# Modulation vectors of a two-layer hybrid block: row products on TensorE replaced by elementwise sums on VectorE and GpSimd and one-column products

## The chip, the cores and the metric

The kernel runs on one core of one Trainium2 chip. The metric is the device time of one execution in microseconds. A core has these engines: TensorE (PE, with its weight loads shown apart as PEld), VectorE (DVE), ScalarE (ACT), GpSimd (POOL) and SyncE (SP, which here issues DMAs). Each works through its own list of instructions in order and waits on semaphores of the others.

## What is computed

Two layers of a hybrid backbone over 1024 latent tokens and 256 context tokens, model width 1024. Each layer has modulation vectors, an input projection, four token mixers, a gated merge of their outputs, an output projection and a layer norm. The parts that matter here are the modulation and the merge:

```python
def modulation(cond, w_mod, b_mod):
    mod = jax.nn.silu(cond) @ w_mod + b_mod
    return jnp.split(mod, 3, axis=-1)

def merge_branches(ys, z, m, w_branch, w_out):
    ...
    acc = sum(jax.nn.sigmoid(ms[i]) * ((ys[i] * jax.nn.silu(zs[i])) @ w_branch[i]) for i in range(N_BRANCH))
    return acc @ w_out

    shift, scale, gate = modulation(c[:, None, :], w_mod, b_mod)
    shift_c, scale_c, gate_c = modulation(c_ctx, w_mod, b_mod)
    p_lat = (layer_norm(x) * (1.0 + scale) + shift) @ w_in
    ...
    x_new = layer_norm(DEEPNORM_ALPHA * x + gate * out) * ln_g + ln_b
```

`w_mod` is 1024 x 3072 per layer, in float32, and there are two condition rows: `c` for the latent tokens and `c_ctx` for the context. The product is thus of two rows by a matrix of 12 MB per layer.

## The kernel before

Shift and scale of layer 0 are needed at the very start and are computed there. The rest is done later, by a generator `later_mods` (L1161): the gate of layer 0 (1024 columns), shift and scale of layer 1 (2048 columns) and the gate of layer 1 (1024 columns). `later_mods` is woven by `weave` (L83, called at L1008) into the merge of layer 0, the stage whose tiles have the prefix `merge`: `weave` takes the next step of the stream that is least far along by its count of steps, 96 for the merge and 68 for the modulations. The merge of layer 1 has no such stream beside it.

**The old modulation** (`modulation`, L173). Each step loads a block of `w_mod`, 128 rows by 512 columns, 256 KB, into a tile with the tag `q` (three buffers). TensorE multiplies it by the two columns of `sc` for these rows (the SiLU of the conditions, 128 rows by 2), with `sc` as weights, in four column groups (L188). The eight row blocks accumulate in PSUM, in the tile `mod__pm`. There the result lies as two rows by many columns. So at the end ScalarE copies each piece to SBUF (L194), TensorE transposes it by 128 columns (L197), and VectorE adds the bias (L199). The tile `modc` then has one column per 128 channels for each condition.

**The merge** (`merge`, L979). The four branches come in the order 2, 3, 1, 0. For each there are eight column blocks c of 128 channels, and for each of those three token groups of 256, 512 and 512. A step multiplies the branch's input u by a 256-row piece of `w_branch` into one third of the PSUM tile `wide`. Where c is even, the gate's logits are computed by TensorE as well (`mm_b`, L307 to L309, three fp32r products for one f32 product: high by high, high by low, low by high). Where c is odd, they were computed earlier and are loaded (L992, `merge__tmp<-start__gates`). ScalarE takes the sigmoid (L996), VectorE multiplies (L1002), and the product is added into the accumulator `acc` (L1003), by GpSimd where c is odd and by VectorE where it is even.

The input u of a branch is loaded in six pieces (`load_u`, L963, with the DMA at L973): two column blocks by three token groups. The pieces land in tiles of the pool `tmp`, which the merge's gates and products use too, so a load waits until such a tile is released; ScalarE and VectorE split each piece into a high and a low part (`hi_lo`, L312 and L313: `merge__uh`, `merge__ul`).

**What sets the order.** Within an engine the program's order is decided when the kernel is built, by a scheduler that places the instructions of the woven streams by when it expects their inputs and their tiles to be free. Nearly all loads here are issued by SyncE, in one queue in program order: a load that waits for its tile holds up those behind it. After the merge, the gate of layer 0 is written to DRAM by two scatter DMAs (L1014, `last__gate<-mod__modc`), and these too are placed among the merge's loads, as soon as the gate is there.

## Time and profile before

| | us |
|---|---|
| median of three runs | 2957.4 (2956.92 to 2962.73) |
| profiled execution | 2960.92 |
| its span | 2959.1 |
| TensorE busy in the span | 2790.4 (94%) |
| VectorE, ScalarE | 1508.0 (51%), 1219.0 (41%) |
| GpSimd | 418.8 (14%) |
| mean granted clock of TensorE | 0.977 |

TensorE is the engine that is busy nearly all the time. A busy engine's own list decides the time only where it doesn't stop, so the stretch of the merge of layer 0 (from about 1090 to 1504 us) is read by itself. In the group rows the last part of a line is the time that the engine stood idle just before these instructions, with what ended it. In the timeline that is the bracket. In the windows a granted clock of 1.00 is TensorE's full speed.

### The profile page before, as it was taken

The page shows a single profiled execution, that of the slowest core. Times are in us where ns is not written, and L with a number is a line of the kernel's source. Part 1 is how long each engine was busy: PE and PEld are TensorE (multiplying, and loading weights), DVE is VectorE, ACT ScalarE, POOL GpSimd, SP SyncE. Part 2 cuts the span into 40 slices and gives each one's busy share as a digit, 9 for nine tenths or more (in the row PEclk, how much of TensorE's full clock was granted, in tenths as well). Part 3 has the DMA queues.
Part 4 walks back from the last instruction along what each step waited for, and adds up shares of the span by engine and source line. Part 5 has one row for each costly group of instructions (what it writes and reads, how often), then busy time and mean ns, then how long its engine had stood idle before and what let it go on. Part 6 is the DMA issues. An engine that isn't in the chain of part 4 may idle for free.

```text
span 2959.1 us, 40218 instructions
## 1 busy us (share of the span) xinstructions
PE 2790.4 (94%) x14458; PEld 2253.0 (76%) x14458; DVE 1508.0 (51%) x3069; ACT 1219.0 (41%) x2631; POOL 418.8 (14%) x507
## 2 busy tenths in 40 slices
PE   7997979999999999899999798999999999999998
PEld 3785858888888887677767576778888888777776
DVE  5644266555555552232458554356555556533456
ACT  4344256445455542222234434346545455522230
POOL 1210020110111100111222120012111111001131
PEclk9998989999999999999999898999999999999999
DMA  6333322222223333333332333423222323222232
GB/s 248 115 107 102 107 72 84 84 84 87 88 88 123 103 98 111 104 120 104 124 98 90 91 103 111 117 74 102 80 93 78 106 103 126 87 94 87 86 109 91
DMA packets 240424, 301.83 MB, mean 102 GB/s; under 512 B 27488, under 2 KB 160096, under 8 KB 240224
## 3 DMA queue, kind: packets, MB, share of 16 engines
q1 hardware_dynamic: 134368, 225.58, 24.2%
q10 hardware_dynamic: 105856, 73.68, 8.0%
q8 instruction: 114, 1.87, 0.3%
q14 instruction: 86, 0.70, 0.1%
HBM read 217.11 MB, written 82.07 MB: 101 GB/s over the span
## 4 chain that ended last, share of the span: by engine, by line
PE 75%; DVE 7%; DMA 4%; ACT 4%; issue 2%; POOL 2%; ACTq 1%; SPq 0%; DVEq 0%; POOLq 0%
PE wide L639 6%; PE merge__mm L307 4%; PE merge__mm L308 4%; PE merge__mm L309 4%; PE wide L307 3%; PE wide L308 3%; PE wide L309 3%; PE m_att__t L584 3%; PE g_att__t L584 2%; PE a_att__mm L307 2%; PE a_att__mm L308 2%; PE a_att__mm L309 2%; PE m_att__mm L309 2%; PE m_att__mm L308 2%; PE m_att__mm L307 2%
## 5 line engine op out<-in xcount | busy, mean ns | idle before, releaser
L307 PE MATMUL merge__mm<-xh,merge__whi 128*128 128x512 f32 (+1 forms) x640 | 243.0, 380 | 0.9 <-ACT a_att__tmp L934 0.9
L308 PE MATMUL merge__mm<-xl,merge__whi 128*128 128x512 f32 (+1 forms) x640 | 239.6, 374 | 0.0
L309 PE MATMUL merge__mm<-xh,merge__wlo 128*128 128x512 f32 (+1 forms) x640 | 239.4, 374 | 0.0
L313 DVE TENSOR_TENSOR m_att__pl<-m_att__t,m_att__ph 128x384 fp32r<-128x384 f32 (+1 forms) x248 | 122.1, 508 | 117.2 <-ACT m_att__ph L312 78.8
L263 ACT CAST merge__whi<-merge__wraw 128x256 fp32r<-128x256 f32 (+1 forms) x128 | 65.6, 513 | 255.6 <-PE merge__mm L308 176.7
L1002 DVE TENSOR_TENSOR merge__tmp<-wide,merge__tmp 128x512 f32<-128x512 f32 (+1 forms) x120 | 76.5, 637 | 184.8 <-PE wide L309 161.2
L1003 POOL TENSOR_TENSOR merge__acc<-merge__acc,merge__tmp 128x512 f32<-128x512 f32 (+1 forms) x60 | 79.2, 1320 | 585.9 <-DVE merge__tmp L1002 585.8
L307 PEld LDWEIGHTS merge__mm<-xh,merge__whi 128*128 128x128 f32 x640 | 120.6, 188 | 44.5 <-issue 19.9
L312 ACT CAST m_att__ph<-m_att__t 128x384 fp32r<-128x384 f32 (+1 forms) x248 | 105.0, 439 | 115.3 <-PE m_att__t L584 103.5
L313 DVE TENSOR_TENSOR g_att__pl<-g_att__t,g_att__ph 128x384 fp32r<-128x384 f32 (+1 forms) x228 | 111.3, 514 | 79.6 <-ACT g_att__ph L312 58.4
L307 PE MATMUL wide<-merge__uh,merge__whi 128*128 128x256 f32 (+1 forms) x320 | 127.4, 398 | 20.4 <-ACT merge__uh L312 11.5
L264 DVE TENSOR_TENSOR merge__wlo<-merge__wraw,merge__whi 128x256 fp32r<-128x256 f32 (+1 forms) x128 | 71.0, 555 | 141.2 <-ACT merge__whi L263 134.3
L309 PEld LDWEIGHTS merge__mm<-xh,merge__wlo 128*128 128x128 f32 x640 | 120.8, 189 | 23.9 <-issue 0.4
L308 PEld LDWEIGHTS merge__mm<-xl,merge__whi 128*128 128x128 f32 x640 | 120.8, 189 | 22.3
L312 ACT CAST g_att__ph<-g_att__t 128x384 fp32r<-128x384 f32 (+1 forms) x228 | 97.7, 446 | 69.3 <-PE g_att__t L584 65.3
L307 PE MATMUL a_att__mm<-xh,a_att__whi 128*128 128x512 f32 (+1 forms) x320 | 123.8, 387 | 0.0
L641 DVE TENSOR_SCALAR_CACHE_REDUCE m_att__p<-wide 128x1280 f32<-128x1280 f32 (+1 forms) x72 | 98.7, 1371 | 42.1 <-PE wide L639 41.8
L309 PE MATMUL a_att__mm<-xh,a_att__wlo 128*128 128x512 f32 (+1 forms) x320 | 120.1, 377 | 0.0
L639 PE MATMUL wide<-g_att__ks,g_att__q 128*128 128x512 f32 (+1 forms) x400 | 103.5, 365 | 17.5 <-DVE g_att__p L641 16.3
L308 PE MATMUL a_att__mm<-xl,a_att__whi 128*128 128x512 f32 (+1 forms) x320 | 120.0, 375 | 0.0
L299 PE MATMUL a_proj__mm<-a_proj__whi,xh 128*128 128x256 f32 (+1 forms) x320 | 112.0, 351 | 8.1 <-ACT a_proj__tmp L809 4.5
L308 PE MATMUL wide<-merge__ul,merge__whi 128*128 128x256 f32 (+1 forms) x320 | 119.6, 374 | 0.0
(418 smaller groups left out, 7919.4 us busy)
## 6 DMA issues: line engine op xcount, KB each, us to landing
merge__wraw<-in_w_chunks_dram SPq DMA_DIRECT2D x64, 256.0 KB, 2.9
mod__wm<-in_w_mod_dram SPq DMA_DIRECT2D x64, 256.0 KB, 3.0
g_proj__wm<-in_w_mod_dram SPq DMA_DIRECT2D x16, 512.0 KB, 9.8
a_att__wraw<-in_w_chunks_dram SPq DMA_DIRECT2D x32, 256.0 KB, 2.7
merge__wraw<-in_w_branch_dram SPq DMA_DIRECT2D x64, 128.0 KB, 2.1
merge__tmp<-start__gates SPq DMA_DIRECT2D x32, 256.0 KB, 3.2
merge__tmp<-outp__gates SPq DMA_DIRECT2D x32, 256.0 KB, 3.4
g_att__wraw<-in_w_chunks_dram SPq DMA_DIRECT2D x28, 256.0 KB, 2.7
```

The source lines that it names most:

```text
L264: (pool if by_pool else dve).tensor_sub(lo[:, :n], raw[:, :n], hi[:, :n])
L299: pe.matmul(ps, xh, wh[:, n0:n1], start=first and k == 0, stop=False)
L307: pe.matmul(ps, wh, xh, start=first and k == 0, stop=False)
L308: pe.matmul(ps, wh, xl, start=False, stop=False)
L309: pe.matmul(ps, wl, xh, start=False, stop=last and k == nk - 1)
L312: act.copy(hi, src)
L313: dve.tensor_sub(lo, src, hi)
L584: pe.transpose(tb[:, i * 128:(i + 1) * 128], pts[q0 + i][:, col:col + 128], ident)
L639: pe.matmul(wide[:, c0:c0 + w], qs[:, j, qi * 128:(qi + 1) * 128], k[:, c0:c0 + w], start=j == 0, stop=j == len(ks) - 1)
L641: dve.tensor_scalar(pt[:, :nk], wide[:, :nk], -scale, None, ALU.mult, ALU.min, accum_out=nb)
L1002: dve.tensor_mul(sgm[:, :g[1]], pb[:, :g[1]], sgm[:, :g[1]])
L1003: (pool if w is None else dve).tensor_add(acc[c][:, gs], acc[c][:, gs], sgm[:, :g[1]])
```

## The change

`later_mods` calls a new function, `modulation_apart`, for all three. The same blocks of `w_mod` are loaded, in another order: now all eight row blocks of 512 columns, then the next 512 columns. Each is multiplied by one number per row (the SiLU of the condition for that row) and the eight products are summed element by element. VectorE does that for the first condition in one instruction per block (L225), GpSimd for the second in two, a scaling into the tile `rb` and an add (L227, L228). The sum over the 128 rows is then left to TensorE: each 128 columns of the sum are the weights of one product with a single column of constants −0.5 (L233), whose result is one column in PSUM, already as `modc` wants it. VectorE multiplies by −2 and adds the bias (L236). The two sums use tiles that other stages own, `ph` with three buffers and `pl` with two. The stream now has 75 steps in place of 67, and its count in `weave` is 76 in place of 68. Lines behind the new function are 36 higher in the new kernel: L973 is L1009, L992 is L1028, L1003 is L1039 and L1014 is L1050.

```diff
@@ -199,6 +199,42 @@
         dve.tensor_tensor(mc[:, :, :n].rearrange("p s n -> p n s"),
                           tps[:, :2 * n].rearrange("p (n s) -> p n s", s=2),
                           bm[:, :n, None].to_broadcast([128, n, 2]), ALU.add)
+        if n == 16:
+            dve.tensor_scalar(mc[:, :, 8:16], mc[:, :, 8:16], 1.0, None, ALU.add)
+        out["m"] = mc
+        yield
+
+    def raw_w():
+        return tp.tile([128, 512], F32, tag="q", name=nm("wm"), bufs=3)
+
+    def modulation_apart(l, base, ncols, out):
+
+        acc = ps_v.tile([128, 512], F32, tag="pv", name=nm("pm"))
+        n = ncols // 128
+        bm = lc.tile([128, 16], F32, tag="bm", name=nm("bm"))
+        sp.dma_start(bm[:, :n], a["b_mod"][l, :, base // 128:base // 128 + n])
+        for h in range(ncols // 512):
+            sums = [tp.tile([128, 512], F32, tag=tag, name=nm("ms"), bufs=b) for tag, b in (("ph", 3), ("pl", 2))]
+            for k in range(KC):
+                w = raw_w()
+                sp.dma_start(w, a["w_mod"][l, k * 128:(k + 1) * 128, base + h * 512:base + (h + 1) * 512])
+                if k == 0:
+                    dve.tensor_scalar(sums[0], w, sc[:, k, 0:1], None, ALU.mult)
+                    pool.tensor_scalar(sums[1], w, sc[:, k, 1:2], None, ALU.mult)
+                else:
+                    dve.scalar_tensor_tensor(sums[0], w, sc[:, k, 0:1], sums[0], ALU.mult, ALU.add)
+                    p = tp.tile([128, 512], F32, tag="rb", name=nm("mp"), bufs=1)
+                    pool.tensor_scalar(p, w, sc[:, k, 1:2], None, ALU.mult)
+                    pool.tensor_tensor(sums[1], sums[1], p, ALU.add)
+                yield
+            for s in range(2):
+                for c in range(4):
+                    o = s * n + 4 * h + c
+                    pe.matmul(acc[:, o:o + 1], sums[s][:, c * 128:(c + 1) * 128], mhalf[:, 0:1], start=True, stop=True)
+            yield
+        mc = lc.tile([128, 2, 16], F32, tag="modc", name=nm("modc"), bufs=4)
+        dve.scalar_tensor_tensor(mc[:, :, :n], acc[:, :2 * n].rearrange("p (s n) -> p s n", s=2), -2.0,
+                                 bm[:, None, :n].to_broadcast([128, 2, n]), ALU.mult, ALU.add)
         if n == 16:
             dve.tensor_scalar(mc[:, :, 8:16], mc[:, :, 8:16], 1.0, None, ALU.add)
         out["m"] = mc
@@ -1005,7 +1041,7 @@
 
         for _ in fill["gen"]:
             pass
-        weave((f"merge{l}", merge(), 4 * KC * len(qgroups)), (f"mod{l}", side, 68))
+        weave((f"merge{l}", merge(), 4 * KC * len(qgroups)), (f"mod{l}", side, 76))
 
 
         phase[0] = f"last{l}"
@@ -1155,13 +1191,10 @@
     ctx.push(pools)
     x1 = dr.tile([SEQ, D], F32, name="x1", bufs=1)
 
-    def raw_w():
-        return tp.tile([128, 512], F32, tag="q", name=nm("wm"), bufs=3)
-
     def later_mods():
-        yield from modulation(0, 2048, 1024, gate0, raw_w, 512)
-        yield from modulation(1, 0, 2048, mc1, raw_w, 512)
-        yield from modulation(1, 2048, 1024, gate1, raw_w, 512)
+        yield from modulation_apart(0, 2048, 1024, gate0)
+        yield from modulation_apart(1, 0, 2048, mc1)
+        yield from modulation_apart(1, 2048, 1024, gate1)
 
     def fin0(t, Y, later):
         if t >= CT:
```

Three places show how the order moves. The first is GpSimd at the last boundary between two branches of the merge: before, its list there holds the accumulator adds of column blocks 5 and 7 of the third branch and nothing else.

```order
L1003 TENSOR_TENSOR merge__acc_11450<-merge__acc_11450,merge__tmp_12922 128x256
L1003 TENSOR_TENSOR merge__acc_11450<-merge__acc_11450,merge__tmp_12936 128x512
L1003 TENSOR_TENSOR merge__acc_11450<-merge__acc_11450,merge__tmp_12947 128x512
L1003 TENSOR_TENSOR merge__acc_11624<-merge__acc_11624,merge__tmp_13096 128x256
L1003 TENSOR_TENSOR merge__acc_11624<-merge__acc_11624,merge__tmp_13135 128x512
L1003 TENSOR_TENSOR merge__acc_11624<-merge__acc_11624,merge__tmp_13153 128x512
```

Now the scalings (L227) and adds (L228) of the last sum, `ms_13692`, stand between the adds into the accumulator of column block 7 (`acc_11668`). The sum's first scaling (L223) and one add are ahead of the excerpt. L223 waits until TensorE has read the sum two before it, whose buffer this sum takes.

```order
L228 TENSOR_TENSOR mod__ms_13692<-mod__ms_13692,mod__mp_13770 128x512
L227 TENSOR_SCALAR mod__mp_13846<-mod__wm_13843,sc 128x512
L1039 TENSOR_TENSOR merge__acc_11668<-merge__acc_11668,merge__tmp_13255 128x256
L228 TENSOR_TENSOR mod__ms_13692<-mod__ms_13692,mod__mp_13846 128x512
L227 TENSOR_SCALAR mod__mp_13869<-mod__wm_13866,sc 128x512
L228 TENSOR_TENSOR mod__ms_13692<-mod__ms_13692,mod__mp_13869 128x512
L1039 TENSOR_TENSOR merge__acc_11668<-merge__acc_11668,merge__tmp_13269 128x512
L227 TENSOR_SCALAR mod__mp_13886<-mod__wm_13883,sc 128x512
L228 TENSOR_TENSOR mod__ms_13692<-mod__ms_13692,mod__mp_13886 128x512
L227 TENSOR_SCALAR mod__mp_13903<-mod__wm_13900,sc 128x512
L228 TENSOR_TENSOR mod__ms_13692<-mod__ms_13692,mod__mp_13903 128x512
L1039 TENSOR_TENSOR merge__acc_11668<-merge__acc_11668,merge__tmp_13289 128x512
```

The three adds into `acc_11668` followed each other directly; now more than two steps of the modulation stand ahead of the first of them, and one and a half to two between each and the next.

The second is SyncE's queue at the same boundary, with the loads of u for the last branch (`start__u_23`). Before, two modulation loads stand between the first and the second piece, and the rest of u follows together.

```order
L992 DMA merge__tmp_13135<-start__gates_18_120 128x512
L992 DMA merge__tmp_13153<-start__gates_18_120 128x512
L973 DMA merge__tmp_13166<-start__u_23_125 128x256
L185 DMA mod__wm_13340<-in_w_mod_dram 128x512
L185 DMA mod__wm_13355<-in_w_mod_dram 128x512
L973 DMA merge__tmp_13170<-start__u_23_125 128x512
L973 DMA merge__tmp_13174<-start__u_23_125 128x512
L973 DMA merge__tmp_13180<-start__u_23_125 128x256
L278 DMA merge__wraw_13505<-in_w_branch_dram 128x256
L973 DMA merge__tmp_13184<-start__u_23_125 128x512
L973 DMA merge__tmp_13188<-start__u_23_125 128x512
```

Now modulation loads stand ahead of the first and behind it, and other loads lie between the pieces; each modulation load waits for the scaling by GpSimd of the block three before it.

```order
L220 DMA mod__wm_13866<-in_w_mod_dram 128x512
L1028 DMA merge__tmp_13289<-start__gates_18_120 128x512
L314 DMA merge__wraw_13532<-in_w_branch_dram 128x256
L220 DMA mod__wm_13883<-in_w_mod_dram 128x512
L1009 DMA merge__tmp_13302<-start__u_23_125 128x256
L220 DMA mod__wm_13900<-in_w_mod_dram 128x512
L220 DMA mod__wm_13994<-in_w_mod_dram 128x512
L1009 DMA merge__tmp_13306<-start__u_23_125 128x512
L171 DMA outp__gt_14159<-last__gate_14084 128x1024
L1009 DMA merge__tmp_13310<-start__u_23_125 128x512
L1009 DMA merge__tmp_13316<-start__u_23_125 128x256
```

The third is SyncE's queue at the first boundary, where the branch after it gets its u (`start__u_26`). Before, the gate's scatter stands between the second and the third piece.

```order
L973 DMA merge__tmp_11680<-start__u_26_128 128x256
L973 DMA merge__tmp_11684<-start__u_26_128 128x512
L180 DMA mod__bm_13147<-in_b_mod_dram 128x8
L1014 DMA last__gate_13919<-mod__modc_11666 128x8x1 x2
L278 DMA merge__wraw_12015<-in_w_branch_dram 128x256
L973 DMA merge__tmp_11688<-start__u_26_128 128x512
L973 DMA merge__tmp_11694<-start__u_26_128 128x256
L973 DMA merge__tmp_11698<-start__u_26_128 128x512
L185 DMA mod__wm_11869<-in_w_mod_dram 128x512
L973 DMA merge__tmp_11702<-start__u_26_128 128x512
```

Now the scatter has moved behind all six, and ahead of the weights and gate logits of the following column block.

```order
L1009 DMA merge__tmp_11725<-start__u_26_128 128x256
L220 DMA mod__wm_12491<-in_w_mod_dram 128x512
L314 DMA merge__wraw_12073<-in_w_branch_dram 128x256
L220 DMA mod__wm_12587<-in_w_mod_dram 128x512
L1009 DMA merge__tmp_11729<-start__u_26_128 128x512
L1009 DMA merge__tmp_11733<-start__u_26_128 128x512
L220 DMA mod__wm_12628<-in_w_mod_dram 128x512
L215 DMA mod__bm_13281<-in_b_mod_dram 128x8
L220 DMA mod__wm_12669<-in_w_mod_dram 128x512
L1050 DMA last__gate_14084<-mod__modc_11697 128x8x1 x2
L314 DMA merge__wraw_12126<-in_w_chunks_dram 128x512
L1028 DMA merge__tmp_11887<-start__gates_11_113 128x256
```

The scatter went from the middle of the u loads to the head of the loads behind them.

## Rows read from the trace of the kernel before

**Rows 1.** Stretches: length, busy PE, PEld, DVE, ACT, POOL (instructions), clock, DMA share, GB/s
```profile
1092.00:1504.00 412.00, 396.97 (x1950) 295.20 (x1950) 143.68 (x246) 111.01 (x236) 57.03 (x52) 0.99 0.38 116
1203.00:1210.00 7.00, 6.50 (x19) 4.48 (x19) 3.43 (x7) 2.51 (x6) 0.00 (x0) 0.66 0.18 54
```

**Rows 2.** Groups by line and shape, TensorE, 1030 to 1510 us; last a weight load
```profile
L188 PE MATMUL mod__pm<-mod__wm,sc 128*2 128x512 f32 x64 | 22.5, 592 | 0.0
L307 PE MATMUL wide<-merge__uh,merge__whi 128*128 128x256 f32 x64 | 20.7, 324 | 13.9 <-ACT merge__uh L312 8.8 <-DVE merge__tmp L1002 5.1
L188 PE MATMUL mod__pm<-mod__wm,sc 128*2 128x256 f32 x128 | 18.7, 378 | 0.0
...
L584 PE MATMUL a_att__t<-ident,a_att__pa 128*128 128x128 f32 x64 | 11.8, 278 | 0.0
...
L197 PE MATMUL mod__t<-ident,mod__tmp 2*128 2x2 f32 x32 | 3.7, 204 | 1.1 <-ACT mod__tmp L194 1.1
...
L309 PEld LDWEIGHTS merge__mm<-xh,merge__wlo 128*128 128x128 f32 x378 | 71.5, 189 | 12.4 <-issue 0.4
```

**Rows 3.** TensorE's timeline around one group of old products: start, duration, [idle before]
```profile
1181.63 0.39 PE L308 MATMUL wide<-merge__ul,merge__whi 128*128 128x512 f32 x1
1181.86 0.39 PE L309 MATMUL wide<-merge__uh,merge__wlo 128*128 128x512 f32 x1
1182.17 0.60 PE L188 MATMUL mod__pm<-mod__wm,sc 128*2 128x256 f32 x4
1182.70 0.39 PE L307 MATMUL merge__mm<-xh,merge__whi 128*128 128x256 f32 x1
```

**Rows 4.** DMA issues, 1186 to 1210 us: count, KB each, us to landing
```profile
last__gate<-mod__modc SPq DMA_DIRECT2D x2, 4.0 KB, 11.1
```

**Rows 5.** Timeline around the long stop: SyncE's queue, then TensorE
```profile
1189.37 1.16 SPq L1014 DMA_DIRECT2D last__gate<-mod__modc  x2
...
1191.89 1.69 SPq L973 DMA_DIRECT2D merge__tmp<-start__u  x3
...
1203.49 0.58 PE L307 MATMUL wide<-merge__uh,merge__whi 128*128 128x256 f32 x1 [7.65 <-ACT merge__uh L312]
```

**Rows 6.** DMA issues, 1280 to 1310 us (the next branch)
```profile
merge__tmp<-start__u SPq DMA_DIRECT2D x4, 256.0 KB, 3.1
```

**Rows 7.** TensorE's timeline: f32 transposes of 128x128, then of two rows
```profile
802.88 0.49 PE L584 MATMUL m_att__t<-ident,m_att__p 128*128 128x128 f32 x3
...
1396.47 0.40 PE L197 MATMUL mod__t<-ident,mod__tmp 2*128 2x2 f32 x4
```

**Rows 8.** Groups by line and shape, GpSimd, whole span
```profile
L1003 POOL TENSOR_TENSOR merge__acc<-merge__acc,merge__tmp 128x512 f32<-128x512 f32 x48 | 70.3, 1465 | 275.4 <-DVE merge__tmp L1002 275.3
...
L264 POOL TENSOR_TENSOR a_att__wlo<-a_att__wraw,a_att__whi 128x512 fp32r<-128x512 f32 x32 | 41.3, 1291 | 2.8 <-PE m_att__mm L309 0.3
...
L261 POOL CAST m_att__whi<-m_att__wraw 128x512 fp32r<-128x512 f32 x28 | 17.1, 611 | 295.6 <-PE m_att__mm L308 176.6 <-PE g_att__mm L308 119.0
```

**Rows 9.** Groups by line and shape, VectorE, 1030 to 1510 us
```profile
L466 DVE SCALAR_TENSOR_TENSOR a_att__y<-a_att__y,a_att__tmp 128x512 f32<-128x512 f32 x2 | 1.4, 692 | 0.1
```

**Rows 10.** Timeline: GpSimd and VectorE at the same time
```profile
1487.98 2.03 POOL L1032 TENSOR_TENSOR xl<-merge__acc,xh 128x256 fp32r<-128x256 f32 x2 [1.20 <-ACT xh L1031]
...
1488.19 1.22 DVE L1003 TENSOR_TENSOR merge__acc<-merge__acc,merge__tmp 128x512 f32<-128x512 f32 x1
```

**Rows 11.** Timeline of the last branch boundary: TensorE, GpSimd, TensorE
```profile
1395.67 0.28 PE L307 MATMUL wide<-merge__uh,merge__whi 128*128 128x256 f32 x1
...
1406.16 1.67 POOL L1003 TENSOR_TENSOR merge__acc<-merge__acc,merge__tmp 128x512 f32<-128x512 f32 x1 [2.53 <-DVE merge__tmp L1002]
...
1410.39 0.39 PE L307 MATMUL wide<-merge__uh,merge__whi 128*128 128x256 f32 x1 [0.54 <-ACT merge__uh L312]
```

**Rows 12.** Groups by line, TensorE, 1395.67 to 1410.39 us
```profile
L197 PE MATMUL mod__t<-ident,mod__tmp 2*128 2x2 f32 x12 | 1.2, 202 | 0.0
L188 PE MATMUL mod__pm<-mod__wm,sc 128*2 128x256 f32 x8 | 1.2, 378 | 0.0
```

## The prediction

> **What bounds the kernel now.** I read first the busy times in the stretch that the change touches, then TensorE's groups by shape there, whose last column gives the stops, then the longest stop in the timeline, and last the loads in front of it. In the merge of layer 0 (about 1090 to 1504 us) TensorE is busy 397.0 of 412 us, VectorE 143.7, GpSimd 57.0 [rows 1]. The stage therefore ends with TensorE's own list of instructions, plus its stops. The groups by shape hold 15.0 us of stops: 13.9 us before the first branch product of a column block (8.8 released by ScalarE's rounding of u, 5.1 by VectorE), and 1.1 us before the transposes [rows 2]. Half of the 15.0 is one stop of 7.65 us at 1203.49 us, where the second branch begins [rows 5], released by the rounding of u. On SyncE's queue the scatter of the gate (`last__gate`, two DMAs) was issued at 1189.37, and the rest of those u loads directly behind it at 1191.89 [rows 5]. The scatter took 11.1 us to land [rows 4]; at the next branch, without it, u lands in 3.1 us [rows 6].
>
> **What is removed from TensorE.** The 96 two-row products leave 192 records, so an f32 matmul runs in two passes. Their busy time is 22.5 + 18.7 us, the transposes take 3.7, and their stop 1.1 [rows 2]: 46.0 us. One group checks it: L308 to L309 is 0.23 us, so the next product of that kind would follow L309 (1181.86) at 1182.09, but behind the four L188 records L307 starts at 1182.70 [rows 3]: 0.61 us for one group of 256 columns, against 18.7/32 = 0.58 by the sum. The ScalarE copies and three small VectorE adds lie beside a busy TensorE and are worth nothing.
>
> **What is added to TensorE.** Eight sums, two condition rows, four blocks of 128 columns: 64 products with 128x128 weights and one moving column, two passes each, so 128 weight loads with next to nothing behind them. No row shows such a product. The nearest is the f32 transpose with a 128x128 operand (L584): three in 0.49 us [rows 7] at a mean of 0.28 for one [rows 2] are (0.49 − 0.28)/2 = 0.11 us apart. The lower bound is the two-row transposes, four in 0.40 us [rows 7] at 0.20 for one [rows 2]: 0.065 us apart. The upper bound is a weight load that nothing overlaps, 0.19 us (L309 on PEld) [rows 2]. I take the f32 transpose: 14.1 us, between 8.3 and 24.3. Entering and leaving each of 16 groups is taken at 0.2 us (in [rows 3] the 0.61 is 0.08 more than the 0.53 from the group's start to the next product; as much again for the turn back, rounded up): 3.2 us. TensorE's list gets shorter by 46.0 − 14.1 − 3.2 = **28.7 us** (18 to 35).
>
> **What is added to VectorE.** 8 tensor_scalar and 56 scalar_tensor_tensor of 128x512 at 0.69 us [rows 9] make 44 us. VectorE then holds 188 of 412 us; it is in order, though, so a step whose weight block has not landed holds up the products behind it. That is counted below, with the loads.
>
> **What is added to GpSimd.** 64 scalings and 56 adds of 128x512. No row shows the scaling; the nearest with one full input is the cast, 0.61 us, and the dearest it can be is the two-input add. The add is the operation of L1003: 1.29 us at its quickest (as L264), 1.47 on the mean of 48 [rows 8], 1.67 in the slow case of [rows 11]. A step costs between 0.61 + 1.29 = 1.9 us and 1.67 + 1.67 = 3.3; with the cast and the slow add it is 2.3, with a quick and a slow add 3.0. Contention is seen on both sides: while GpSimd works off two L1032, VectorE's L1003 takes 1.22 us [rows 10] where its 128x512 operations take 0.69 [rows 9]. I take 2.35 us. In all 64 × 2.35 = 150 us, which beside the 57 is 207 of the 384 us of a stage that is 28 us shorter: on the average GpSimd has room, so the question is where it works in bursts.
>
> It does come in bursts. The sums on GpSimd's side have two buffers, so sum h may start only when TensorE has read sum h−2. By the order, TensorE's products stand at each half branch: at the boundaries and in the middle. Behind each product GpSimd finds eight steps, and between them stand the accumulator adds of the odd column block that ends the old branch (excerpt of GpSimd). Those adds release the buffers into which the next branch's u is loaded. SyncE's queue puts modulation loads, each waiting for GpSimd's scaling of the block three earlier, between those u loads (excerpt of SyncE). So after the product at a branch boundary, the u of its second column block comes only behind about six scalings, six adds, and three accumulator adds.
>
> At the last boundary, from the product of column block 0 to the first use of that u, TensorE took 1410.39 − 1395.67 = 14.7 us [rows 11]; without the 0.54 us stop in front and the 2.4 us of modulation [rows 12] that is 11.8 us of work. GpSimd's work is 6 steps plus about 2.2 us of adds, then a load of 3.1 [rows 6] and a cast of some 0.6 (as GpSimd's, [rows 8]): 17.3 us with a step of 1.9; 20.0 with 2.35; 24 with 3.0. TensorE stops for 5.5, **8.2** or 12. At the boundary before it there is one add less in the way: 4, **6.7**, 10.5. At the first boundary the gate's scatter no longer stands between the u loads, so the 7.65 goes; but it now stands ahead of a weight load and the gate loads of the next column block, and u is behind GpSimd there too: 5, **7**, 11. In mid-branch and for the last pair of products: 1, **2**, 6. Of the other 7.35 us of stops now, I leave 4.6 that belong to no boundary. Sum 20, **28.5**, 44, against 15.0 now.
>
> **Clock.** Behind the 7.65 us stop the granted clock was 0.66 in the next 7 us [rows 1], between TensorE's two levels of 2.4 GHz (1.00) and 1.2 GHz (0.50): 7 × 0.34 = 2.4 us lost. One such dip is in the time now. With three stops of 6 to 8 us there would be at most two more: +3 us taken (1 to 5).
>
> **Sum.** −28.7 + 13.5 + 3 = −12.2 us. The profiled execution took 2960.9 us, 3.5 above the median of 2957.4; taken off the median: 2945, and with 2 us for VectorE's waits for late weight blocks, which I could not price by the row, **2947**. With the cheap step −28.7 + 5 + 1 = −23: 2935. With the dear one −28.7 + 29 + 4 = +4: 2962, and with dear products (24.3 us) on top 2972.
>
> **A rule weighed against the rows.** [Rows 10] show VectorE's add at 1.22 us beside GpSimd's, 0.53 longer than [rows 9], which is part of the length of what GpSimd ran. The Trainium skill ("SBUF — State Buffer", section "Terms") says that VectorE with two SBUF inputs and GpSimd contend for one pair of ports under an exclusive lock, held for the whole instruction, so that the loser blocks fully. By that, each scalar_tensor_tensor that meets a GpSimd add would delay it by its whole length, and the other way round. The row fits a block for part of an instruction; no row says how often the two would meet. The result by the rule is rival C.
>
> **Rivals.**
> A. GpSimd is quick or its bursts fall into slack: TensorE alone decides. The step is 1.9 us or less, the first boundary loses its stop of 7.65 with the dip of 2.4, and the others keep what they have: −28.7 − 10 = −39 at best, 2919; with one or two stops of some 3 to 5 us left, 2922 to 2930. For it: GpSimd is busy 57 of 412 us now. Against: the order shows u behind the steps. 0.24.
> B. The forecast, 2930 to 2954, likeliest 2947. 0.37.
> C. VectorE and GpSimd block each other for whole instructions: a GpSimd step costs 0.61 + 1.29 + 0.69 = 2.6 us, and VectorE's up to 0.69 + 1.29. Two boundaries cost 6 × 0.25 = 1.5 us more each than in B, the first and the middle 1 more each, and VectorE's late products some 3: +8, 2954 to 2961, no measurable difference. 0.20.
> D. Slower: GpSimd's burst decides at every boundary. The place is the u of the second column block. Each 0.1 us of step is 0.6 us at each of three boundaries, 1.8, and with half as much again for VectorE behind late weight blocks and for the clock 2.7 us; so the −12 at 2.35 is eaten at a step of 2.8, and at 3.2 it is −12 + 8.5 × 2.7 = +11: 2968. For it: adds take up to 1.67 now, and the scaling is unseen. Against: a cast of the same width takes 0.61. 0.18.
> E. The change doesn't do what it says, in that the products cost TensorE more than the old ones. They would need 128 loads at over 0.33 us, more than a load that nothing overlaps. 0.01.
>
> **The numbers.** The likeliest is B with 2947. Eight in ten reach from the middle of A, 2925, to the middle of D, 2967; B's own range is 2930 to 2954. What a measurement of this kernel can tell from no change is about 0.2%, 6 us: below 2951.5 is faster, above 2963.3 slower. A and most of B (0.24 + 0.32) make faster 0.56; the rest of B, C and D's lower edge 0.05 + 0.18 + 0.02 = 0.25; the rest of C and D with E 0.02 + 0.16 + 0.01 = 0.19.
>
> **What would show it.** Right: L197 and L188 are gone from the merge; the 64 products show some 14 us; the step on GpSimd is near 2.3 us; TensorE's longest stops stand at the second, third and fourth branch's second column block, released by ScalarE's rounding of u behind DMA behind GpSimd; `last__gate` no longer stands before the longest stop. A is shown by stops under 12 us in the stage; C by VectorE's scalar_tensor_tensor at 1.0 us and more on the mean; D by a GpSimd step over 2.8 us. It is wrong if TensorE stops for its own products (the sum of GpSimd not ready), which I put at under 2 us, at the last pair only, or if stages outside this merge change.

## The result: slower by 2.4%, and the profile after

The changed kernel took 3029.9 us (median of four; 3028.1 to 3031.0) against 2958.3 us: a ratio of 1.0239, 95% interval 1.0226 to 1.0251. The forecast was 2947 us, with a range of 2925 to 2967 us. The time came out 83 us above the forecast and on the other side of no change.

It is all in the merge of layer 0, which by the distance from its first product to the last took 414.6 us before and 489.2 us now. The rest of the kernel took 2544.5 us before and 2537.0 now in the profiled executions, and 2536 to 2549 in those of all the runs here, so a few us between two kernels can come from outside the stage. This is the stage's stretch in the new kernel, with the columns of [rows 1]:

```profile
1092.00:1576.00 484.00, 396.49 (x1838) 325.14 (x1837) 202.28 (x304) 106.49 (x223) 239.75 (x168) 0.90 0.33 100
```

GpSimd went from 57 of 412 us to 240 of 484, TensorE's clock from 0.99 to 0.90 of full speed. TensorE's groups there answer to [rows 2]:

```profile
L343 PE MATMUL wide<-merge__uh,merge__whi 128*128 128x512 f32 x128 | 57.4, 448 | 36.2 <-DVE merge__tmp L1038 25.7 <-DVE merge__acc L1036 8.9 <-ACT merge__uh L348 1.5
...
L343 PE MATMUL wide<-merge__uh,merge__whi 128*128 128x256 f32 x64 | 22.5, 352 | 49.7 <-ACT merge__uh L348 21.9 <-DVE merge__tmp L1038 15.6 <-DVE merge__acc L1036 12.2
...
L233 PE MATMUL mod__pm<-mhalf,mod__ms 128*128 128x1 f32 x128 | 17.9, 269 | 0.0
```

The stops before branch products are 36.2 and 49.7 us, with 2.5 us before others 88.4, against 15.0. The new products take 17.9 us of busy time, against the 46.0 that went (1.1 of it a stop). By the distances of starts, the merge's own products took 354.1 us before and 381.0 now: 26.9 us are the slower clock behind all those stops. So: −24 us of TensorE's list, +73.4 of stops, +26.9 of clock, −1.7 of other work make the +74.6 of the stage.

GpSimd's groups, to be read beside [rows 8], where the cast took 611 ns:

```profile
L227 POOL TENSOR_SCALAR mod__mp<-mod__wm,sc 128x512 f32<-128x512 f32 x56 | 98.4, 1757 | 10.3 <-PE a_att__t L500 5.4
L228 POOL TENSOR_TENSOR mod__ms<-mod__ms,mod__mp 128x512 f32<-128x512 f32 x56 | 77.0, 1375 | 4.1
...
L223 POOL TENSOR_SCALAR mod__ms<-mod__wm,sc 128x512 f32<-128x512 f32 x8 | 13.8, 1730 | 110.7 <-PE mod__pm L233 101.7 <-PE a_att__pv L628 9.0
```

The scaling takes 1757 ns, more than the two-input add behind it. A step is 1.76 + 1.38 = 3.13 us. The last row is the first scaling of each sum: GpSimd stood idle 110.7 us in all before these eight, 101.7 of it for TensorE's products. That is the two-buffer burst. One of its beginnings, with TensorE's products in front:

```profile
1328.52 1.84 PE L233 MATMUL mod__pm<-mhalf,mod__ms 128*128 128x1 f32 x16
...
1330.46 1.65 POOL L223 TENSOR_SCALAR mod__ms<-mod__wm,sc 128x512 f32<-128x512 f32 x1 [14.10 <-PE mod__pm L233]
```

The sixteen records take 1.84 us, some 0.105 us apart, as [rows 7] had it. VectorE's share of the sum, and SyncE's waits in the stage (total us, times, longest):

```profile
L225 DVE SCALAR_TENSOR_TENSOR mod__ms<-mod__wm,sc,mod__ms 128x512 f32<-128x512 f32 x56 | 48.9, 873 | 83.4 <-DMA mod__wm<-in_w_mod_dram 83.3
```

```profile
SPq L220 <- POOL mod__mp L227: 123.1, 48, 4.6
SPq L1009 <- POOL merge__acc L1039: 22.1, 6, 5.0
SPq L220 <- POOL mod__ms L223: 20.6, 7, 4.2
```

VectorE stood 83.4 us idle before its steps, for blocks of `w_mod` that hadn't landed; SyncE's queue stood 144 us at modulation loads whose tile GpSimd hadn't released, and 22 us at u loads behind its accumulator adds. The length of such waits is not the price by itself. In the kernel before, SyncE's queue stood nearly as long at modulation loads, for TensorE's own products, beside only 15.0 us of stops:

```profile
SPq L185 <- PE mod__pm L188: 110.4, 35, 7.9
```

What is new is whom the queue waits for. How that stops TensorE is seen in one place, in the timeline of all engines:

```profile
1294.18 1.55 POOL L1039 TENSOR_TENSOR merge__acc<-merge__acc,merge__tmp 128x512 f32<-128x512 f32 x1
1294.23 5.26 SPq L220 DMA_DIRECT2D mod__wm<-in_w_mod_dram  x2
...
1295.69 1.28 POOL L228 TENSOR_TENSOR mod__ms<-mod__ms,mod__mp 128x512 f32<-128x512 f32 x1
...
1297.02 0.77 DVE L225 SCALAR_TENSOR_TENSOR mod__ms<-mod__wm,sc,mod__ms 128x512 f32<-128x512 f32 x1 [2.45 <-DMA mod__wm<-in_w_mod_dram]
1297.07 2.07 POOL L227 TENSOR_SCALAR mod__mp<-mod__wm,sc 128x512 f32<-128x512 f32 x1
...
1298.14 0.40 PE L345 MATMUL merge__mm<-xh,merge__wlo 128*128 128x512 f32 x1
...
1301.88 0.75 DVE L225 SCALAR_TENSOR_TENSOR mod__ms<-mod__wm,sc,mod__ms 128x512 f32<-128x512 f32 x1 [4.08 <-DMA mod__wm<-in_w_mod_dram]
1302.55 0.68 DVE L1038 TENSOR_TENSOR merge__tmp<-wide,merge__tmp 128x512 f32<-128x512 f32 x1
...
1303.28 0.67 PE L343 MATMUL wide<-merge__uh,merge__whi 128*128 128x512 f32 x1 [4.75 <-DVE merge__tmp L1038]
```

SyncE is held at two modulation loads from 1294.23 to 1299.5, while GpSimd does an accumulator add, an add and a scaling. VectorE's next step therefore can't start before 1301.88, after 4.08 us. Behind it in VectorE's list stands the product L1038, which releases a third of `wide`. TensorE, which has nothing else to do, waits for it 4.75 us, to 1303.28.

### The profile page after: what moved, and what is told of

It is laid out like the page before. It is cut to its first block, busy times and chain, and to the rows that moved or that the text cites. A ratio compares the mean times of both kernels' runs of the same rounds, so it can differ in the third digit from the quotient of the medians.

```text
span 3026.2 us, 40271 instructions
## 1 busy us (share of the span) xinstructions
PE 2794.1 (92%) x14362; PEld 2285.1 (76%) x14362; DVE 1570.8 (52%) x3133; ACT 1216.1 (40%) x2619; POOL 606.3 (20%) x627
## 5 line engine op out<-in xcount | busy, mean ns | idle before, releaser
L343 PE MATMUL wide<-merge__uh,merge__whi 128*128 128x256 f32 (+1 forms) x320 | 134.4, 420 | 91.8 <-DVE merge__tmp L1038 44.4
L343 PEld LDWEIGHTS wide<-merge__uh,merge__whi 128*128 128x128 f32 x320 | 63.4, 198 | 129.0 <-DVE merge__tmp L1038 55.8
L1038 DVE TENSOR_TENSOR merge__tmp<-wide,merge__tmp 128x512 f32<-128x512 f32 (+1 forms) x120 | 76.3, 636 | 147.4 <-PE wide L345 143.6
L1039 POOL TENSOR_TENSOR merge__acc<-merge__acc,merge__tmp 128x512 f32<-128x512 f32 (+1 forms) x60 | 80.6, 1343 | 344.9 <-DVE merge__tmp L1038 344.7
L345 PE MATMUL wide<-merge__uh,merge__wlo 128*128 128x256 f32 (+1 forms) x320 | 123.8, 387 | 0.0
```

What stands on the lines that cost most here:

```text
L343: pe.matmul(ps, wh, xh, start=first and k == 0, stop=False)
L345: pe.matmul(ps, wl, xh, start=False, stop=last and k == nk - 1)
L1038: dve.tensor_mul(sgm[:, :g[1]], pb[:, :g[1]], sgm[:, :g[1]])
L1039: (pool if w is None else dve).tensor_add(acc[c][:, gs], acc[c][:, gs], sgm[:, :g[1]])
```

## The experiments

The theories were these. **1**: VectorE, working in order, stands behind sums whose block is late, because GpSimd frees the block's tile only after its own scaling. **2**: GpSimd's accumulator adds come late and hold the tiles for u and the gate logits. **3**: VectorE is too full. **4**: the two-buffer wait makes the bursts. **5**: SyncE's queue, where a modulation load waiting for GpSimd holds up the merge's loads. All times are medians; the kernel before took 2957 to 2959 us beside them, the changed kernel 3029.9. An edit can also make the scheduler set the stage in another order. By the traces the program's order is the same on every engine in the changed kernel, scale_const and scale_copy; in no_vector_sum and copy_no_vector; and in same_blocks and copy_same_blocks. Every other edit here came with an order of its own, so its time holds that too.

**all_vector: the second sum on VectorE too** (likewise at k = 0).

```diff
-                    pool.tensor_scalar(p, w, sc[:, k, 1:2], None, ALU.mult)
-                    pool.tensor_tensor(sums[1], sums[1], p, ALU.add)
+                    dve.scalar_tensor_tensor(sums[1], w, sc[:, k, 1:2], sums[1], ALU.mult, ALU.add)
```

> Both sums on VectorE (64 steps of two operations), none on GpSimd. Theory 1 (VectorE works in order and stands behind sums whose weight block is late, because GpSimd frees the block's tile only after its own scaling; TensorE then finds no free bank): the waits for weight blocks (81.6 + 11.7 us on VectorE in the changed kernel) fall under 15 us, TensorE's stops in the merge of layer 0 fall from 88 to about 15 us, its clock goes back to 0.98 or more, and the time is 2958 - 24 (TensorE's shorter list) - 8 (the stop at the first boundary) = about 2926. Theory 2 (GpSimd's late accumulator adds hold up the loads of u): the same, 2926 to 2935. Rival 3 (VectorE itself is too full: 64 x 2 x 0.75 = 96 us on top of 144): stops stay above 40 us, 2960 to 2990.

Measured 2927.3 us, ratio 0.9901 (0.9884 to 0.9917). The stretch of its merge, and VectorE's two steps there:

```profile
1092.00:1476.00 384.00, 365.92 (x1862) 302.81 (x1862) 220.43 (x360) 108.12 (x224) 57.59 (x51) 0.99 0.42 123
```

```profile
L225 DVE SCALAR_TENSOR_TENSOR mod__ms<-mod__wm,sc,mod__ms 128x512 f32<-128x512 f32 x56 | 47.1, 842 | 7.0 <-DMA mod__wm<-in_w_mod_dram 6.7
L226 DVE SCALAR_TENSOR_TENSOR mod__ms<-mod__wm,sc,mod__ms 128x512 f32<-128x512 f32 x56 | 44.3, 791 | 0.4
```

The clock is back at 0.99, TensorE's stops in the stage are 18.1 us, and VectorE is busy 220 of 384 us and waits 7.0 us for blocks. GpSimd's part is the whole of the loss; theory 3 falls. The same 64 loads are still in SyncE's queue, so their traffic alone isn't the cause either. The theories about how remain.

**no_vector_sum: GpSimd's steps unchanged, VectorE without any.**

```diff
-                    dve.scalar_tensor_tensor(sums[0], w, sc[:, k, 0:1], sums[0], ALU.mult, ALU.add)
...
-                    pe.matmul(acc[:, o:o + 1], sums[s][:, c * 128:(c + 1) * 128], mhalf[:, 0:1], start=True, stop=True)
+                    pe.matmul(acc[:, o:o + 1], sums[1][:, c * 128:(c + 1) * 128], mhalf[:, 0:1], start=True, stop=True)
```

> The first sum is left out (VectorE does no step of it, and the products read the second sum for both conditions); GpSimd has the same steps as in the changed kernel. Theory 1 (VectorE in order behind late weight blocks): the stops released by VectorE's products (62 us of the 88) go, the time falls to 2945 to 2965. Theory 2 (GpSimd's late accumulator adds hold up the loads of u, and with them TensorE): the stops stay near 80 us, 3010 to 3030.

Measured 3009.9 us, 20 less than the changed kernel. Theory 1 alone would have brought 65 to 85. The waits of SyncE and of TensorE:

```profile
SPq L220 <- POOL mod__mp L225: 117.9, 49, 3.7
...
PE wide L341 <- DVE merge__tmp L1036: 40.4, 11, 11.8
PE wide L341 <- ACT merge__uh L346: 25.3, 6, 5.9
```

SyncE still waits 118 us for GpSimd's scaling, and TensorE's stops are still 81.6 us, released by VectorE and ScalarE. ScalarE waits 60.9 us for loads of gate logits and 51.9 for u, much as in the changed kernel (57.9 and 61.3), and VectorE stands behind ScalarE. That is where theory 5 came from.

**scale_const: GpSimd scales by a constant.** `sc[:, k, 1:2]` becomes `0.5` in both of its scalings.

> GpSimd scales by the constant 0.5 in place of the condition's number per row; all else as in the changed kernel. If the 1.76 us of the scaling are the price of one number per row: it falls to 0.6 to 1.0 us, a GpSimd step to 2.1 us, the stops by a third to a half, 2980 to 3000. If they are the price of this operation on GpSimd at 128x512: 1.5 us or more as before, 3020 to 3030.

Measured 3023.5 us, and the scaling

```profile
L227 POOL TENSOR_SCALAR mod__mp<-mod__wm 128x512 f32<-128x512 f32 x56 | 92.5, 1651 | 9.7 <-PE a_att__t L500 5.4
```

is 6% cheaper. The price is that of this operation at this size; one number per row is not what makes it dear.

**three_sums: three tiles for GpSimd's sum.**

```diff
-            sums = [tp.tile([128, 512], F32, tag=tag, name=nm("ms"), bufs=b) for tag, b in (("ph", 3), ("pl", 2))]
+            turn[0] += 1
+            sums = [tp.tile([128, 512], F32, tag=tag, name=nm("ms"), bufs=b)
+                    for tag, b in (("ph", 3), ("rb", 1) if turn[0] % 3 == 0 else ("pl", 2))]
```

> GpSimd's sum takes one of three tiles in turn instead of two (the scaled product moves into the upper half of the weight block's tile, so its old tile is free for a third sum, and the scaled product has three tiles). Theory 4 (the bursts come from the wait for TensorE's product two sums earlier, 101.7 us on GpSimd): that wait falls under 30 us, the steps spread, and the stops halve: 2970 to 3000. Theory 1 in its narrow form (a GpSimd step of 3.1 us holds a block too long, bursts or not): the waits on VectorE stay over 60 us, 3010 to 3035.

Measured 2998.3 us, 32 less. The scaled product `p` moves into the upper half of the block's tile, which frees its old tile for the third sum; a block is then free only behind the add. GpSimd's wait for TensorE's products fell from 101.7 us to

```profile
POOL mod__ms L228 <- PE mod__pm L238: 42.3, 3, 14.1
```

so the two-buffer wait is a part. What it is worth alone this run doesn't show, since it also gives `p` three tiles and holds each block longer.

**same_blocks, acc_on_vector, same_blocks_acc.** The first loads three blocks once and leaves out the other 61 loads:

```diff
-                w = raw_w()
-                sp.dma_start(w, a["w_mod"][l, k * 128:(k + 1) * 128, base + h * 512:base + (h + 1) * 512])
+                if len(blocks) < 3:
+                    blocks.append(raw_w())
+                    sp.dma_start(blocks[-1], a["w_mod"][l, k * 128:(k + 1) * 128, base + h * 512:base + (h + 1) * 512])
+                w = blocks[k % 3]
```

the second has `(pool if w is None and l else dve).tensor_add(acc...)` in L1039, the third has both.

> Three weight blocks are loaded once and used again by every step; the other 61 loads are left out. GpSimd has the same steps and the same accumulator adds. Theory 5 (SyncE's queue: a modulation load that waits for GpSimd's scaling holds up the loads of gates, weights and u behind it): the waits of SyncE for GpSimd's scaling (123 + 21 us) are gone, ScalarE's waits for loads of gates and u (58 + 61 us) fall by more than half, and the time falls to 2935 to 2960. Theory 2 (GpSimd's accumulator adds come late and hold the buffers of gates and u): the stops of TensorE stay over 60 us, 2995 to 3025.

> All accumulator adds of the merge of layer 0 go to VectorE (36 more there, none on GpSimd); the modulation steps and their loads are as in the changed kernel. Theory 2: nothing of the merge waits for GpSimd but through the loads' queue, the stops fall to 20 to 35 us, 2940 to 2960. Theory 5: the stops stay over 60 us, 3000 to 3030. Theory 1 (VectorE in order behind late blocks): 3020 or more, since VectorE has still more behind each late block.

> Both edits together: three blocks loaded once, the other 61 loads left out, and all accumulator adds of the merge of layer 0 on VectorE. GpSimd still does its 64 steps, but only TensorE's products wait for them. Theories 2 and 5: 2925 to 2940, stops of 15 to 30 us. If stops of over 50 us stay, the wait is for the sums themselves (TensorE's products behind GpSimd).

Measured 2989.0, 3018.4 and 2967.7 us: 41, 11.5 and 62 less than the changed kernel. Neither theory 2 nor theory 5 holds alone, and together they fell short of the 2925 to 2940 us that was expected. With both ways closed, 50.1 us of stops are left, 19.3 of them because the sums themselves are late (TensorE's waits in same_blocks_acc, total us, times, longest):

```profile
PE mod__pm L237 <- POOL mod__ms L232: 19.3, 2, 12.5
PE wide L347 <- DVE merge__tmp L1042: 16.9, 9, 10.2
```

**no_vector_acc: no step on VectorE, no accumulator add on GpSimd**, the edits of no_vector_sum and acc_on_vector.

> The first sum is left out (VectorE has no step) and all accumulator adds of the merge of layer 0 are on VectorE. What is left of GpSimd's ways into the merge is SyncE's queue (modulation loads waiting for GpSimd ahead of the merge's loads) and TensorE's wait for the sums. If SyncE's queue is worth some 20 us on top of what same_blocks_acc (2967.7) has: 2985 to 3000. If VectorE's wait for blocks and the accumulator adds were all: 2965 to 2972.

Measured 3000.9 us. It differs from same_blocks_acc in having the loads in SyncE's queue and no sum on VectorE, and is 33 us slower. The loads cost that much there, although VectorE has less to do. Through which wait the run doesn't show; SyncE's queue, which stands 147 us for GpSimd in it, is the likely one.

**scale_scalar: ScalarE scales, GpSimd only adds.** The scalings become `act.activation(p, w, AF.Identity, scale=sc[:, k, 1:2])`, with `p` in the upper half of the block's tile.

> ScalarE does the scaling for the second sum (into the upper half of the block's tile), GpSimd only the add; VectorE as in the changed kernel. A GpSimd step is then the add of 1.3 to 1.4 us, less than half of 3.1. Theories 2 and 5 both give a stop in proportion to the burst: 35 to 45 us of stops, 2955 to 2975. If ScalarE, in order, stands behind late blocks as VectorE does, 2990 or more.

Measured 2951.5 us, ratio 0.9979 (0.9967 to 0.9991): 78 less than the changed kernel, for 1.76 us off GpSimd's step, and better than expected.

**scale_copy, copy_no_vector, copy_same_blocks: GpSimd's step at the price that was forecast.** `pool.tensor_copy(p, w)` replaces the scaling, which leaves the condition's factor out; the other two add the edits of no_vector_sum and of same_blocks.

> GpSimd copies the block in place of scaling it (the condition's factor is left out of the second sum); all else as in the changed kernel. The copy's rows before were 0.61 us, so a step is about 2.0 us, which is what the prediction supposed. If the prediction failed only in the price of the scaling: 2935 to 2955. If its reckoning of what a burst costs was too small as well: 2965 to 3000.

> GpSimd copies in place of scaling (its step about 2.3 us), and VectorE's sum is left out, the products reading GpSimd's sum twice. Against scale_copy (2979.0): if VectorE's waits for late weight blocks are the missing 32 us, 2945 to 2955; if SyncE's queue is, 2968 to 2980; if half and half, about 2962.

> GpSimd copies in place of scaling, and only three weight blocks are loaded, which all steps use. VectorE's late blocks and SyncE's waits for GpSimd are both gone; the accumulator adds behind GpSimd's steps stay, which is what the prediction reckoned with: 2940 to 2952 if that reckoning was right for its own part, 2960 or more if the burst before the accumulator adds itself was reckoned too low.

Measured 2979.0, 2952.8 and 2963.2 us. GpSimd's groups and VectorE's step and wait for blocks in scale_copy, and the stretch of copy_no_vector:

```profile
L228 POOL TENSOR_TENSOR mod__ms<-mod__ms,mod__mp 128x512 f32<-128x512 f32 x56 | 81.0, 1446 | 3.9
L227 POOL COPY mod__mp<-mod__wm 128x512 f32<-128x512 f32 x56 | 47.7, 852 | 8.9 <-PE a_att__t L500 5.4 <-DMA mod__wm<-in_w_mod_dram 0.5
...
L225 DVE SCALAR_TENSOR_TENSOR mod__ms<-mod__wm,sc,mod__ms 128x512 f32<-128x512 f32 x56 | 63.0, 1125 | 27.0 <-DMA mod__wm<-in_w_mod_dram 26.7
...
DVE mod__ms L225 <- DMA mod__wm<-in_w_mod_dram: 26.0, 25, 3.2
```

```profile
1092.00:1504.00 412.00, 378.37 (x1846) 312.21 (x1847) 157.33 (x246) 106.78 (x224) 173.16 (x169) 0.95 0.39 117
```

The step is 0.85 + 1.45 = 2.30 us, the forecast's 2.35, and the time is still 32 us over the forecast. Without VectorE's sum 26 of these go. In the third, SyncE's and VectorE's waits for blocks are gone, but VectorE's 64 operations stay, and so do the accumulator adds behind the bursts: 16 go. TensorE's stops released by the rounding of u are three there, one at each boundary between branches:

```profile
PE wide L347 <- ACT merge__uh L352: 22.0, 3, 8.4
```

With the order the same, the dear step against the cheap one is worth 51 us in the changed kernel, 57 without VectorE's sum (3009.9 against 2952.8) and 26 with the loads left out (2989.0 against 2963.2). So the length of GpSimd's step is what most of the loss comes from, and about half of what it costs goes through the loads, if the other order of same_blocks is worth little.

**all_vector_gate, old_gate, all_vector_rows, old_rows: the gate's scatter.** The first two issue it by `act.dma_start`; the others turn the gate on TensorE first:

```diff
+        gps, grow = tbank(), tmp()
         for s in range(2):
-            sp.dma_start(gd[s].rearrange("(k p) -> p k", p=128), gate["m"][:, s, :KC])
+            pe.transpose(gps[0:KC, s * 128:(s + 1) * 128], gate["m"][:, s, :KC], ident)
+        act.copy(grow[0:KC, :256], gps[0:KC, :256])
+        for s in range(2):
+            sp.dma_start(gd[s].rearrange("(k p) -> k p", p=128), grow[0:KC, s * 128:(s + 1) * 128])
```

> All on VectorE as in all_vector (2927.3 us), and the gate's scatter is issued by ScalarE in place of SyncE. In all_vector two stops of 5.1 and 4.9 us at the first boundary (1191 to 1214 us) have the two scatter DMAs just ahead of the loads they wait for. If the place in SyncE's queue is what costs: both stops go and the time is 2915 to 2920. If the scatter's many small pieces hold up the DMA engines whichever queue they come from: no change, 2925 to 2929.

> The kernel before with one change, the gate's scatter issued by ScalarE. If its place in SyncE's queue makes the 7.65 us stop: about 7.65 + 2.4 us (clock) less, 2946 to 2951. If not: 2955 to 2960.

> all_vector (2927.3 us) with the gate turned by TensorE (two small transposes) and copied, so that it goes to DRAM in 16 pieces of 512 bytes rather than 2048 of 4. If the many small pieces make the two stops of 5 us at the first boundary: 2914 to 2920. If the stops there have another cause: 2925 to 2930.

> The kernel before with the gate written in 16 pieces of 512 bytes rather than 2048 of 4. If the small pieces make the 7.65 us stop: 2946 to 2951, and the u loads at the first boundary land in about 3 us. If not: 2956 to 2960.

Measured: all_vector_gate 2925.8 us (ratio 0.9898, 0.9877 to 0.9919) and old_gate 2958.0 (0.9999, 0.9989 to 1.0009), both no different from the same kernel with the scatter on SyncE. The DMA issues at the first boundary in old_gate, to be read beside [rows 4]:

```profile
merge__tmp<-start__u SPq DMA_DIRECT2D x4, 256.0 KB, 6.8
...
last__gate<-mod__modc ACTq DMA_DIRECT2D x2, 4.0 KB, 11.5
```

On another queue the scatter takes as long, and u is still held: a stop of 7.02 us stands where there were 7.65. Then all_vector_rows 2919.8 us (0.9876, 0.9848 to 0.9903), and old_rows 2953.6 (0.9978, 0.9966 to 0.9991), which is less than the 2946 to 2951 that was to show the small pieces. In old_rows u lands in

```profile
merge__tmp<-start__u SPq DMA_DIRECT2D x4, 256.0 KB, 3.0
```

and the stop is 0.25 us. But the write isn't at that boundary any more. It stands behind the transposes and the copy now, and in the order that came of it, at the end of the stage:

```profile
1487.97 0.66 SPq L1018 DMA_DIRECT2D last__gate<-last__tmp  x2
```

In all_vector_rows it stands at 1457.92 us. So the scatter beside the u loads is what costs, whichever queue it is in. That the size of its pieces is the reason is likely (4 KB took 11 us), but these runs changed its place together with its pieces and don't show it. all_vector_rows beats both kernels; the stretch of its merge:

```profile
1092.00:1460.00 368.00, 359.73 (x1841) 297.06 (x1840) 216.97 (x354) 107.54 (x223) 58.16 (x51) 1.00 0.39 123
```

TensorE's stops in the stage are 8.7 us, and the stage is 372.4 us long.

## Why the prediction was wrong, by its own steps

**What is removed, and the products: right.** −46.0 us are gone; the products were forecast at 14.1 + 3.2 = 17.3 us and took 16.8 by the distances of starts. TensorE's list got 24 us shorter by that measure, 28.7 forecast; the rest of the difference is that the old groups were 41 by the distances and not 46.

**GpSimd's step: wrong, and the first failed step.** It took the scaling's price so: "the nearest with one full input is the cast, 0.61 us, and the dearest it can be is the two-input add." The scaling took 1.76 us, above that bound. The step was 3.13 us where 2.35 was taken, though inside the range of 1.9 to 3.3. What it was worth is the difference between scale_copy and the changed kernel: 3029.9 − 2979.0 = 51 us for 0.83 us of step, 6.1 us for each 0.1, where rival D reckoned 2.7. The order of the program is the same in both. VectorE's own steps got longer beside the copies (873 to 1125 ns), so the 51 us are, if anything, too few. D had the sign, and less than half of the slope: at 3.13 it gives 2966. Its place, the u of the second column block, holds the smaller part of the stops, as is seen below.

**VectorE and the loads behind GpSimd's step: the second failed step.** The text named it ("a step whose weight block has not landed holds up the products behind it") and then gave it 2 us, since no row showed it. In the changed kernel 62.4 of the 88.4 us of stops were released by products on VectorE (L1038, L1036, by the rows above), all along the branches. At the forecast's own step of GpSimd, leaving VectorE's sum out is worth 2979.0 − 2952.8 = 26 us, and leaving the loads out 16. At the dear step it is 20 and 41. So the loads cost more the longer the step is. VectorE's sum does not, though its waits for blocks are 83 us at the dear step and 27 at the cheap one, so the 26 us are not the price of late blocks alone. How they divide between late blocks and the 64 operations themselves stays open. The forecast looked at the loads of u in SyncE's queue, and not at the loads of gates and weights, which stand behind the same waiting modulation loads. The two failed terms and a remainder, 51 + 26 − 2 + 8, make up the 83 us. That the remainder is only 8 us (copy_no_vector at 2952.8 against the forecast of 2945 without the 2 us) is partly luck: the stage took 414.3 us there against 414.6 before, where the forecast had some 12 less.

**The bursts at the boundaries: there, no larger than forecast, and not where most of the time went.** The forecast had 7 + 6.7 + 8.2 = 21.9 us of stops at the three boundaries. At its own step of GpSimd, the rounding of u released 12.0 us of stops in scale_copy, and 22.0 with the loads left out, so what copy_same_blocks lost over the forecast isn't there. In the changed kernel the three are 16.6, though the step is dearer:

```profile
1223.60 0.58 PE L343 MATMUL wide<-merge__uh,merge__whi 128*128 128x256 f32 x1 [4.86 <-ACT merge__uh L348]
...
1354.72 0.58 PE L343 MATMUL wide<-merge__uh,merge__whi 128*128 128x256 f32 x1 [6.03 <-ACT merge__uh L348]
...
1474.86 0.58 PE L343 MATMUL wide<-merge__uh,merge__whi 128*128 128x256 f32 x1 [5.75 <-ACT merge__uh L348]
```

The accumulator adds, on which the sum was built, are worth 11.5 us alone and 21 with the blocks in place.

**Clock: wrong in size.** +3 us taken, +26.9 measured. It was counted for three long stops; there were some thirty, most of 1 to 6 us, and the mean clock of the stage fell to 0.90.

**The scatter: half right.** It moved from between the u loads, but stops stayed at the first boundary. old_gate shows that its place in SyncE's queue wasn't the cause, and old_rows that the stop goes when the scatter is not there. In the changed kernel this is lost in the rest.

**Rival C, blocking between VectorE and GpSimd: there, and not what makes the changed kernel slow.** In the changed kernel's timeline:

```profile
1342.27 1.27 POOL L228 TENSOR_TENSOR mod__ms<-mod__ms,mod__mp 128x512 f32<-128x512 f32 x1
1342.39 1.71 DVE L300 TENSOR_TENSOR merge__wlo<-merge__wraw,merge__whi 128x512 fp32r<-128x512 f32 x1
```

A VectorE subtraction of 128x512 took 1.71 us beside GpSimd's add, where the same operation took 0.68 at 1329.40 us. The Trainium skill ("SBUF — State Buffer", "Terms") has the loser blocked for the whole instruction of the other; this row is near that. In the changed kernel VectorE's steps took 873 ns on the mean against 750 for one alone, 7 us in all 56. In scale_copy they took 1125, which is over the 1.0 us that the prediction set as the sign of C, so a part of the 26 us above can be C's; no run separates it. But they are longer still in scale_scalar,

```profile
L226 DVE SCALAR_TENSOR_TENSOR mod__ms<-mod__wm,sc,mod__ms 128x512 f32<-128x512 f32 x56 | 66.5, 1188 | 21.1 <-DMA mod__wm<-in_w_mod_dram 20.6
```

which is 78 us faster than the changed kernel.

What stays open: how much of the cost of the loads goes through late blocks on VectorE and how much through SyncE's queue; how the last 40 us between same_blocks_acc and all_vector divide (19.3 us of waits for sums, a slower clock, and VectorE's slowed operations are seen there); and whether the gate's scatter in larger pieces would leave u alone at its old place.

## What to carry to other kernels

Work moved to an engine with room is not free if the engine holds something that the busy engines wait for: follow each tile that it reads to the load that refills it, and that load's queue to what stands behind it. Of an operation without a row, the bound should be as wide as the doubt; here a second reader of the same tile, 3.13 us a step beside 0.87, cost 103 us against all_vector, and the same work on one faster engine gained 30. What no row shows and the text names as a mechanism needs a price from both sides, and not a rounding.

## What the runs showed of the hardware

GpSimd's tensor_scalar of 128x512 in float32 took 1.65 us on the mean with a constant and 1.76 with a number per row, where its copy of the same size took 0.61 alone and 0.85 in scale_copy, and its two-input add 1.38. VectorE's scalar_tensor_tensor of that size took 0.75 us alone, 0.87 on the mean beside GpSimd's scalings and adds, and 1.13 beside its copies and adds. Two DMAs of 4 KB each in pieces of 4 bytes (2080 packets on their queue in old_gate) took 11 us to land, and loads of 256 KB beside them took 6.8 us, with the two on another queue as well, where such loads took 3.0 without them.
